# A hybrid decoder layer on one core: the second half's residual norm in the middle of the first FFN block, its steps and the second norm one block further to the front

## The chip, the cores and the metric

The kernel runs on one core of a Trainium2 chip. The metric is the device time of one execution in microseconds (us), lower is better; a median over several executions is given where there are several. A core has TensorE (PE, matmuls, with its weight loads shown as PEld), VectorE (DVE), ScalarE (ACT), GpSimd (POOL) and SyncE (SP), which here only issues transfers. Each engine works through a queue of its own in order, and waits on semaphores for the others.

## The reference

One layer over a sequence of 1024 positions of width 1024, in float32. A token mixer with three branches (pooling, RWKV-7, attention into a memory) gives `merged`; then come an output projection, two norms and a gated feed-forward network with a causal convolution of width 3:

```python
x = x + rms_norm(merged @ w_o[l], norm_mix_post[l])

h = rms_norm(x, norm_ffn_pre[l])
u = causal_dwconv(h @ w_ffn_up[l], conv_w[l], conv_b[l])
u_gate, u_val = jnp.split(u, 2, axis=-1)
f = (jax.nn.gelu(u_gate, approximate=True) * u_val) @ w_ffn_down[l]
x = x + rms_norm(f, norm_ffn_post[l])
```

`rms_norm` divides each position by the root of its mean square over the 1024 channels. The feed-forward width is 2816 for the gate and 2816 for the value. The change lies between the output projection and the first blocks of the feed-forward network.

## The kernel before

Everything is kept transposed: channels on the 128 partitions, positions along the row. The 1024 positions are worked on in two halves of 512 (index n); the 1024 channels are 8 chunks of 128 (index k). Each float32 operand of a matmul is split into a high and a low part, and a product takes three matmuls (`mm3`, lines 163 to 171: high by high, low by high, high by low). A block of the feed-forward's first matrix is 128 output columns for one half: `gemm` (L173) runs 8 chunks of three matmuls, 24 in all, into one PSUM bank.

Weights come through `load_w`: SP loads 128x256 pieces (L158), ScalarE casts the high part (L129) and GpSimd subtracts for the low part (L132). A block has four pieces. Two classes of buffers alternate between blocks, three raw and four split pieces each. So a cast for a block can only run when the matmuls of the block two before it have read the piece in that place.

`up_block` (L978) is one such block and its convolution: ScalarE scales the bank and adds the bias (L962), VectorE adds the two shifted products (L963, L964). Block j below `NF` (22) is a gate block, block `NF` + j its value block. `up_act` (L984) takes the GELU of a gate block, multiplies by the value block and stores the product.

Between the output projection of a half (`wo_gemm`) and its feed-forward blocks stand two norms. `wo_residual(n, after)` is a generator: it asks TensorE for the sum over channels of the squares that `wo_gemm` has collected (L1097 in `norm`, a matmul by a matrix of 1/1024), takes the inverse root on ScalarE (a logarithm and an exponential, both L200), and then for each chunk scales on VectorE (L1140), adds x (L1142), stores the result to `d_x1` on SP (L1143) and adds its square to a second sum (ScalarE L1091, VectorE L1092). It yields after every second chunk, so it has four steps, the first of which includes the norm. `wo_norm(n, s2, after)` is the second norm: again a matmul (L1097) and an inverse root, then for each chunk a scaling (L1159), a cast to the high part (L122) and a subtraction for the low part (L123), the operands `h2h[n]` and `h2l[n]` of the feed-forward blocks of half n. It yields after every second chunk too. In both, `after` keeps the norm's matmul behind a given matmul in TensorE's queue.

The code around the change (L1191 to L1223) runs feed-forward blocks of half 0 while the norms of half 1 go on. The order is: block one (gate 0); norm of the residual, chunks 0 and 1; block two (value 0); chunks 2 and 3; block three (gate 1); chunks 4 and 5; block four (value 1); chunks 6 and 7; blocks five and six (gate 2, value 2); the weights of two blocks ahead; the second norm and its first step; the load of the GELU table; then blocks seven to ten (gate and value 3 and 4), with the gate products of pairs 0, 1 and 2 and the other three steps of the second norm behind blocks seven, eight and nine, and the last two gate products at the end. After that come the five block pairs of half 1 (`early`), which need all of `h2h[1]`, with `differences(k)` (L1252 to L1257, VectorE subtractions L1255 and splits) between them; they prepare operands for the 17 remaining pairs, which use a Strassen-like scheme (`up_pair`), and then comes the second matrix.

This program order is not the order of the queues. The framework that builds the program puts each engine's instructions in order by their place in the program and by when it thinks their inputs are there; `later` and `after` add fixed orders.

Of the kernel before, what the change touches and what calls it, by code (L numbers as in the profile page):

```python
# [20 lines left out]
KC = D // P  # L21
# [7 lines left out]
NF = 22  # L29
# [15 lines left out]
def trunk_kernel(ctx: ExitStack, tc: tile.TileContext, xT, memT, pvec, w_in, w_kv, w_upd, w_upg,  # L45
# [98 lines left out]
    def load_w(ap, nk, kp=2, c=None):  # L144
        if c is None:
            cls[0] ^= 1
            c = cls[0]
        ps = Ws()
        ps.c = c
        for k0 in range(0, nk, kp):  # L150
            load_more(ps, ap, k0, min(kp, nk - k0), kp)
        return ps

    def load_more(ps, ap, k0, n, kp):
        raw = wp.tile([P, kp, P], F32, name="wraw", tag=f"wraw{ps.c}", bufs=3)
        hi = wp.tile([P, kp, P], FR, name="whi", tag=f"whi{ps.c}", bufs=4)
        lo = wp.tile([P, kp, P], FR, name="wlo", tag=f"wlo{ps.c}", bufs=4)
        SP.dma_start(raw[:, :n], ap[:, k0:k0 + n])  # L158
        split_w(raw[:, :n], hi[:, :n], lo[:, :n])
        for j in range(n):  # L160
            ps.append((hi[:, j], lo[:, j]))

    last_mm = [None]

    def mm3(ps, w, x, start, stop):
        wh, wl = w
        xh, xl = x
        first = PE.matmul(ps, wh, xh, start=start, stop=False)  # L168
        PE.matmul(ps, wh, xl, start=False, stop=False)  # L169
        last_mm[0] = PE.matmul(ps, wl, xh, start=False, stop=stop).ins  # L170
        return first

    def gemm(ws, rhs, width=512, behind=None, ps=None, log=None):  # L173

        if ps is None:
            ps = psg.tile([P, 512], F32, name="psg", tag=f"g{getattr(ws, 'c', 0)}")[:, :width]
        n = len(ws)
        for k in range(n):
            m = mm3(ps, ws[k], rhs(k), k == 0, k == n - 1)
            if k == 0 and behind is not None:  # L180
                later(m, behind)
            if log is not None:
                log.append(last_mm[0])
        return ps


# [44 lines left out]
    first = [Ws(), Ws()]  # L231
# [522 lines left out]
    with tc.tile_pool(name="km", bufs=1) as km:  # L754
# [31 lines left out]
        for j in range(8):  # L786
            ws = kv_weights(j) if j > 1 else load_w(w_kv[j], KC, c=0)
            ps = gemm(ws, lambda k: (mh[:, k], ml[:, k]), 256)
# [61 lines left out]
    for hd in range(4):  # L850
        for t0, _ in HALVES:
# [7 lines left out]
            for u in range(2):  # L859
                ps = psg.tile([P, 2, 256], F32, name="psco", tag="g0")  # L860
# [41 lines left out]
    for j in range(8):  # L902
        ws = load_w(w_pmem[j], 4)
        for n, (t0, _) in enumerate(HALVES):
# [3 lines left out]
            ps = gemm(ws, lambda k: (oh[k][:, s], ol[k][:, s]))  # L908
            V.tensor_tensor(pm[j][n], pm[j][n], ps, op=ALU.mult)
    for j in range(8):  # L910
        ws = load_w(w_ppool[j], 4)
# [3 lines left out]
        for n, (t0, _) in enumerate(HALVES):  # L915
            s = slice(t0, t0 + 512)
            ps = gemm(ws, lambda k: (ph_[k][:, s], pl_[k][:, s]))
# [39 lines left out]
    def conv(j, n, src, d):  # L957

        if n == 0:
            zcs[j] = const.tile([P, 2], F32, name="zc2", tag="zc2", bufs=16)  # L960
        zc = zcs[j]
        A.activation(d, src, AF.Identity, scale=col("cw2", j), bias=col("cb", j))  # L962
        V.scalar_tensor_tensor(d[:, 1:], src[:, :511], col("cw1", j), d[:, 1:], op0=ALU.mult, op1=ALU.add)  # L963
        V.scalar_tensor_tensor(d[:, 2:], src[:, :510], col("cw0", j), d[:, 2:], op0=ALU.mult, op1=ALU.add)  # L964
        if n == 0:
            V.tensor_copy(zc, src[:, 510:512])
        else:
            V.scalar_tensor_tensor(d[:, 0:1], zc[:, 1:2], col("cw1", j), d[:, 0:1], op0=ALU.mult,
                                   op1=ALU.add)
            V.scalar_tensor_tensor(d[:, 0:2], zc, col("cw0", j), d[:, 0:2], op0=ALU.mult, op1=ALU.add)  # L970
# [4 lines left out]
        cnt[e] = (cnt[e] + 1) % 4  # L975
        return pmp.tile([P, 512], F32, name=name, tag=f"n{8 + 4 * e + cnt[e]}")

    def up_block(j, n, ws):  # L978
        e = j // NF
        d = work(e, ("ug", "uv")[e])  # L980
        conv(j, n, gemm(ws, lambda k: (h2h[n][:, k], h2l[n][:, k])), d)
        return d

    def up_act(i, n, ug, uv):  # L984
        act(ug, ug, AF.Gelu_apprx_tanh)
        V.tensor_tensor(ug, ug, uv, op=ALU.mult)
        SP.dma_start(d_f[i][:, n * 512:n * 512 + 512], ug)
# [96 lines left out]
    h2h, h2l = [], []  # L1084
# [40 lines left out]
    def wo_residual(n, after=None):  # L1125

        s = slice(n * 512, n * 512 + 512)
        o = os_[n]
        rs = norm(ow, sss[n], after)
        s2 = ow.tile([P, 512], F32, name="s2", tag="ss", bufs=2)  # L1130
        if n:
            xts = hf.tile([P, KC, 512], F32, name="xts", tag="h2h1")
            SP.dma_start(xts, xT[:, s].rearrange("(k p) t -> p k t", p=P))
        for k in range(KC):
            if n:
                xt = xts[:, k]
            else:
                xt = ow.tile([P, 512], F32, name="xt", tag="xt", bufs=2)
                SP.dma_start(xt, xT[k * P:(k + 1) * P, s])
            V.scalar_tensor_tensor(o[k], o[k], col("g_mix_post", k), rs, op0=ALU.mult,  # L1140
                                   op1=ALU.mult)
            V.tensor_tensor(o[k], o[k], xt, op=ALU.add)  # L1142
            SP.dma_start(d_x1[k][:, s], o[k])  # L1143
            sumsq(s2, o[k], k == 0, V)
            if k % 2:
                yield s2
# [6 lines left out]
    def wo_norm(n, s2, after=None):  # L1153

        o = os_[n]
        rs = norm(ow, s2, after)
        new_h2()
        for k in range(KC):
            V.scalar_tensor_tensor(o[k], o[k], col("g_ffn_pre", k), rs, op0=ALU.mult,  # L1159
                                   op1=ALU.mult)  # L1160
            split(o[k], h2h[n][:, k], h2l[n][:, k], V)
            if k % 2:
                yield
# [13 lines left out]
    res = wo_residual(0, pin)  # L1177
    s2 = next(res)
    table(SIGMOID)
    for j in range(3, 8):  # L1180
        merge(1, range(j, j + 1))
        s2 = next(res, s2)
# [5 lines left out]
    for _ in wo_norm(0, s2, last_mm[0]):  # L1188
        pass
    wo_gemm(1, range(2, 8))  # L1190
    def first(j):  # L1191
        return up_block(j, 0, load_w(w_fup[j], KC))

    pairs = [[first(0)]]
    res = wo_residual(1, last_mm[0])
    s2 = next(res)
    pairs[0].append(first(NF))
    s2 = next(res)
    for i in (1, 2):
        pairs.append([first(i)])  # L1200
        s2 = next(res, s2)
        pairs[i].append(first(NF + i))
        s2 = next(res, s2)

    ahead = [load_w(w_fup[3], KC), load_w(w_fup[NF + 3], KC)]
    steps = wo_norm(1, s2, last_mm[0])
    next(steps)
    table(GELU)
    later(phase[0], last_whi[0], True)
    for n in range(4):  # L1210
        j = (3, NF + 3, 4, NF + 4)[n]
        d = up_block(j, 0, ahead.pop(0))
        if n < 2:
            ahead.append(load_w(w_fup[(4, NF + 4)[n]], KC))
            up_act(n, 0, *pairs[n])
            pairs.append([d])
        else:
            up_act(n, 0, *pairs[n]) if n == 2 else None
            pairs.append([d])
        if n < 3:  # L1220
            next(steps)
    up_act(3, 0, pairs[3][0], pairs[4][0])
    up_act(4, 0, pairs[5][0], pairs[6][0])  # L1223


    o0, o1 = os_
# [137 lines left out]
    log = []  # L1364
# [34 lines left out]
    X, ahead, third = down  # L1399
# [217 lines left out]
```

## Time and profile before

| | |
|---|---|
| median of 3 runs | 2079.53 us (2077.59 to 2079.88) |
| the profiled execution, its own time | 2081.88 us |
| its span, first to last instruction | 2080.0 us |
| mean granted TensorE clock | 0.992 |
| TensorE busy, span | 2014.5 us, 97% |
| VectorE, ScalarE, GpSimd busy | 1361.4, 1069.4, 812.5 us |
| TensorE busy, 1372.0 to 1437.6 (half 0's ten blocks) | 61.92 of 65.60 us |
| TensorE busy, 1437.6 to 1500.0 (half 1's ten blocks) | 55.46 of 62.40 us |

The profile is one execution. Times in it are in us from the first instruction. In a row of an engine's queue stand the start, the length, the engine, the line of the kernel, the operation, the tile written and the tiles read, the shapes, how many instructions were joined (x2), and in brackets how long the engine was idle before it and what that wait ended with. In a row by stretches, each engine has its busy time and its number of instructions. Matmuls overlap: one is shown as 0.39 us long, but they start about 0.23 us apart. Tiles of the text have these names there: `psn` is the bank of a norm, `psg` that of a block, `ss` the first sum of squares, `s` the second, `rs` the inverse root, `ug` and `uv` the outputs of gate and value blocks, `o` the output projection and later the residual, `whi`, `wlo` and `wraw` the split and the raw weights.

### The profile page before, as it was taken

The page shows a single profiled execution, that of the slowest core. Times are in us where ns is not written, and L with a number is a line of the kernel's source. Part 1 is how long each engine was busy: PE and PEld are TensorE (multiplying, and loading weights), DVE is VectorE, ACT ScalarE, POOL GpSimd, SP SyncE. Part 2 cuts the span into 40 slices and gives each one's busy share as a digit, 9 for nine tenths or more (in the row PEclk, how much of TensorE's full clock was granted, in tenths as well). Part 3 has the DMA queues.
Part 4 walks back from the last instruction along what each step waited for, and adds up shares of the span by engine and source line. Part 5 has one row for each costly group of instructions (what it writes and reads, how often), then busy time and mean ns, then how long its engine had stood idle before and what let it go on. Part 6 is the DMA issues. An engine that isn't in the chain of part 4 may idle for free.

```text
span 2080.0 us, 34125 instructions
## 1 busy us (share of the span) xinstructions
PE 2014.5 (97%) x12246; PEld 1558.7 (75%) x12246; DVE 1361.4 (65%) x2170; ACT 1069.4 (51%) x2249; POOL 812.5 (39%) x917
## 2 busy tenths in 40 slices
PE   8999999999999999999999999998999999989997
PEld 5777767776778667866878878876678777767886
DVE  6567437664667357823895443778777777767798
ACT  7585348623773367434566243546444443444644
POOL 5521213121222121212133355655588888832341
PEclk9999999999999999999999999999999999999999
DMA  4312211120212021214427343634322222169776
GB/s 155 130 41 74 67 59 61 65 82 22 87 61 98 24 89 61 78 51 133 160 82 234 123 142 110 213 123 135 109 72 76 79 74 83 64 189 261 166 181 149
DMA packets 176713, 221.83 MB, mean 107 GB/s; under 512 B 16544, under 2 KB 128288, under 8 KB 176544
## 3 DMA queue, kind: packets, MB, share of 16 engines
q1 hardware_dynamic: 163616, 204.44, 30.3%
q0 software_dynamic: 11856, 14.16, 4.2%
q8 instruction: 97, 1.59, 0.3%
q10 hardware_dynamic: 1072, 1.05, 0.2%
q14 instruction: 72, 0.59, 0.1%
HBM read 170.30 MB, written 49.28 MB: 106 GB/s over the span
## 4 chain that ended last, share of the span: by engine, by line
PE 30%; DVE 7%; DMA 5%; POOL 4%; issue 4%; ACT 3%; SPq 0%; POOLq 0%; ACTq 0%; DVEq 0%
PE psg L170 5%; PE psg L169 5%; PE psg L168 5%; POOL wt L1028 2%; PE psd L169 2%; PE psd L170 2%; PE psf L170 2%; PE psd L168 2%; PE psf L169 2%; PE psf L168 2%; POOL sm L1013 1%; DMA a<-in_w_fup 1%; DMA g<-d_zg 1%; DMA R<-d_f 1%; POOL wlo L132 1%
## 5 line engine op out<-in xcount | busy, mean ns | idle before, releaser
L132 POOL TENSOR_TENSOR wlo<-wraw,whi 128x256 fp32r<-128x256 f32 x472 | 411.6, 881 | 941.8 <-ACT whi L129 775.1
L168 PE MATMUL psg<-hh,whi 128*128 128x512 f32 x928 | 380.7, 410 | 2.7 <-DVE kv L315 2.7
L170 PE MATMUL psg<-hh,wlo 128*128 128x512 f32 x928 | 376.9, 406 | 0.2
L169 PE MATMUL psg<-hl,whi 128*128 128x512 f32 x928 | 375.8, 405 | 0.0
L129 ACT CAST whi<-wraw 128x256 fp32r<-128x256 f32 x472 | 182.7, 403 | 220.8 <-PE psg L169 108.0
L168 PEld LDWEIGHTS psg<-hh,whi 128*128 128x128 f32 x928 | 174.7, 188 | 43.3 <-DVE kv L315 4.0
L170 PEld LDWEIGHTS psg<-hh,wlo 128*128 128x128 f32 x928 | 174.5, 188 | 43.2 <-POOL wlo L132 5.3
L169 PEld LDWEIGHTS psg<-hl,whi 128*128 128x128 f32 x928 | 174.7, 188 | 39.5 <-issue 3.4
L1028 POOL TENSOR_TENSOR wt<-a,wt 128x256 fp32r<-128x256 f32 x136 | 133.8, 1013 | 31.3 <-ACT wt L1027 31.3
L168 PE MATMUL psd<-f,u 128*128 128x512 f32 x292 | 115.8, 397 | 8.2 <-ACT f L1355 4.8
L169 PE MATMUL psd<-f,u 128*128 128x512 f32 x292 | 115.6, 396 | 0.6 <-DVE f L1359 0.6
L170 PE MATMUL psd<-f,u 128*128 128x512 f32 x292 | 115.2, 396 | 0.0
L1028 POOL TENSOR_TENSOR wt<-sm,wt 128x256 fp32r<-128x256 f32 x102 | 106.8, 1066 | 19.2 <-ACT wt L1027 19.2
L170 PE MATMUL psf<-h2h,wt 128*128 128x512 f32 x272 | 108.8, 400 | 1.0 <-POOL wt L1028 0.6
L168 PE MATMUL psf<-h2h,wt 128*128 128x512 f32 x272 | 106.3, 391 | 1.7 <-ACT wt L1027 1.6
L169 PE MATMUL psf<-h2l,wt 128*128 128x512 f32 x272 | 106.0, 390 | 0.0
L1027 ACT CAST wt<-sm 128x256 fp32r<-128x256 f32 x102 | 37.9, 404 | 129.4 <-POOL sm L1013 124.1
L1046 DVE SCALAR_TENSOR_TENSOR d<-z,pv,d 128x1023 f32<-128x1023 f32 x68 | 91.6, 1347 | 12.0 <-ACT d L1044 9.5
L170 PE MATMUL psf<-t,wt 128*128 128x512 f32 x204 | 80.8, 396 | 3.4 <-POOL wt L1028 3.4
L686 DVE TENSOR_TENSOR HV<-ph,Hd 64x128 f32<-64x128 f32 x112 | 32.4, 289 | 72.2 <-PE ph L640 48.0
L168 PE MATMUL psf<-t,wt 128*128 128x512 f32 x204 | 79.6, 390 | 0.0
L169 PE MATMUL psf<-t,wt 128*128 128x512 f32 x204 | 79.5, 390 | 0.0
(424 smaller groups left out, 4750.7 us busy)
## 6 DMA issues: line engine op xcount, KB each, us to landing
wraw<-in_w_in SPq DMA_DIRECT2D x240, 128.0 KB, 2.4
a<-in_w_fup SPq DMA_DIRECT2D x128, 128.0 KB, 2.4
d_zg<-st SPq DMA_DIRECT2D x48, 256.0 KB, 2.7
wraw<-in_w_fup SPq DMA_DIRECT2D x80, 128.0 KB, 2.5
fw<-in_w_fdn SPq DMA_DIRECT2D x33, 256.0 KB, 4.2
fraw<-d_f SPq DMA_DIRECT2D x33, 256.0 KB, 5.3
wraw<-in_w_prwkv SPq DMA_DIRECT2D x64, 128.0 KB, 2.4
wraw<-in_w_o SPq DMA_DIRECT2D x64, 128.0 KB, 2.5
```

The lines of the kernel that those rows point to most:

```text
L129: last_whi[0] = A.copy(hi, src).ins
L132: (V if lo_on_dve[0] else G).tensor_tensor(lo, src, hi.bitcast(F32), op=ALU.subtract)
L168: first = PE.matmul(ps, wh, xh, start=start, stop=False)
L169: PE.matmul(ps, wh, xl, start=False, stop=False)
L170: last_mm[0] = PE.matmul(ps, wl, xh, start=False, stop=stop).ins
L686: ready = V.tensor_tensor(HV[q, :, c + 1, e], ph[q], Hd[q], op=ALU.add).ins
L1013: eng.tensor_tensor(out_[u], a[u], b[u], op=op)
L1027: A.copy(w[0][:, us], src[u])
L1028: last_low[0] = G.tensor_tensor(w[1][:, us], src[u], w[0][:, us].bitcast(F32), op=ALU.subtract).ins
L1046: V.scalar_tensor_tensor(d[:, n:], z[:, :T - n], col(cw, j), d[:, n:], op0=ALU.mult, op1=ALU.add)
```

## The change

`gemm` gets an argument `amid`, a function that it calls behind the matmuls of chunk 3, and `up_block` passes it on. The start of `wo_residual(1)` with its norm and chunks 0 and 1 becomes such a function of block one, and the norm's matmul is kept behind the 12th matmul of the block instead of the 24th. Of the other steps, chunks 2 and 3 now come ahead of block two, 4 and 5 ahead of block three, 6 and 7 ahead of block four. The second norm comes behind block five instead of six: blocks six to ten are now in `queue`, the first two of them (value 2 and gate 3) have their weights loaded ahead, and the gate products of pairs 0, 1 and 2 with the three steps of the second norm follow blocks six, seven and eight. Number, operands and shapes of all operations stay.

```diff
-    def gemm(ws, rhs, width=512, behind=None, ps=None, log=None):
+    def gemm(ws, rhs, width=512, behind=None, ps=None, log=None, amid=None):
...
             if log is not None:
                 log.append(last_mm[0])
+            if amid is not None and k == 3:
+                amid()
         return ps
...
-    def up_block(j, n, ws):
+    def up_block(j, n, ws, amid=None):
         e = j // NF
         d = work(e, ("ug", "uv")[e])
-        conv(j, n, gemm(ws, lambda k: (h2h[n][:, k], h2l[n][:, k])), d)
+        conv(j, n, gemm(ws, lambda k: (h2h[n][:, k], h2l[n][:, k]), amid=amid), d)
         return d
...
-    def first(j):
-        return up_block(j, 0, load_w(w_fup[j], KC))
-
-    pairs = [[first(0)]]
-    res = wo_residual(1, last_mm[0])
-    s2 = next(res)
-    pairs[0].append(first(NF))
-    s2 = next(res)
-    for i in (1, 2):
-        pairs.append([first(i)])
-        s2 = next(res, s2)
-        pairs[i].append(first(NF + i))
-        s2 = next(res, s2)
-
-    ahead = [load_w(w_fup[3], KC), load_w(w_fup[NF + 3], KC)]
-    steps = wo_norm(1, s2, last_mm[0])
+    blocks, s2 = [], [None]
+
+    def first(j, amid=None):
+        blocks.append(up_block(j, 0, load_w(w_fup[j], KC), amid))
+
+    def begin():
+        res.append(wo_residual(1, last_mm[0]))
+        s2[0] = next(res[0])
+
+    res = []
+    first(0, begin)
+    for j in (NF, 1, NF + 1, 2):
+        s2[0] = next(res[0], s2[0])
+        first(j)
+
+    queue = (NF + 2, 3, NF + 3, 4, NF + 4)
+    ahead = [load_w(w_fup[j], KC) for j in queue[:2]]
+    steps = wo_norm(1, s2[0], last_mm[0])
     next(steps)
     table(GELU)
     later(phase[0], last_whi[0], True)
-    for n in range(4):
-        j = (3, NF + 3, 4, NF + 4)[n]
-        d = up_block(j, 0, ahead.pop(0))
-        if n < 2:
-            ahead.append(load_w(w_fup[(4, NF + 4)[n]], KC))
-            up_act(n, 0, *pairs[n])
-            pairs.append([d])
-        else:
-            up_act(n, 0, *pairs[n]) if n == 2 else None
-            pairs.append([d])
+    for n, j in enumerate(queue):
+        blocks.append(up_block(j, 0, ahead.pop(0)))
         if n < 3:
+            ahead.append(load_w(w_fup[queue[n + 2]], KC))
+            up_act(n, 0, *blocks[2 * n:2 * n + 2])
             next(steps)
-    up_act(3, 0, pairs[3][0], pairs[4][0])
-    up_act(4, 0, pairs[5][0], pairs[6][0])
+    for n in (3, 4):
+        up_act(n, 0, *blocks[2 * n:2 * n + 2])
```

## The prediction

> **What bounds the kernel now.** I read the page first, then busy time by stretches around the edited code, then the queues of TensorE, VectorE and ScalarE there, and the waits last.
>
> ```profile
> span 2080.0 us, 34125 instructions
> ...
> PE 2014.5 (97%) x12246; PEld 1558.7 (75%) x12246; DVE 1361.4 (65%) x2170; ACT 1069.4 (51%) x2249; POOL 812.5 (39%) x917
> ...
> PE 30%; DVE 7%; DMA 5%; POOL 4%; issue 4%; ACT 3%; SPq 0%; POOLq 0%; ACTq 0%; DVEq 0%
> ```
>
> TensorE is busy for 97% of the span, so only its gaps can be won. The second view gives busy time and counts by stretch; the columns after POOL are granted clock, DMA share and GB/s.
>
> ```profile
> 1372.00:1405.60 33.60, 33.60 (x147) 27.14 (x145) 23.49 (x33) 14.43 (x33) 19.20 (x23) 1.00 0.47 147
> 1405.60:1412.60 7.00, 3.32 (x7) 1.88 (x7) 5.11 (x10) 4.15 (x10) 4.54 (x6) 0.76 0.59 191
> 1412.60:1437.60 25.00, 25.00 (x112) 20.53 (x110) 20.33 (x31) 15.59 (x32) 13.58 (x14) 1.00 0.48 147
> 1437.60:1460.00 22.40, 18.55 (x73) 13.01 (x73) 22.09 (x30) 12.89 (x29) 14.61 (x15) 1.00 0.27 88
> 1460.00:1480.00 20.00, 18.64 (x77) 13.63 (x76) 18.61 (x28) 9.61 (x23) 11.77 (x15) 1.00 0.36 114
> ```
>
> Two stretches lose TensorE time: 1405.6 to 1412.6, and 1437.6 to 1480, where VectorE is busy for 40.7 of 42.4 us. TensorE's own queue shows the first:
>
> ```profile
> 1372.03 0.39 PE L168 MATMUL psg<-h2h,whi 128*128 128x512 f32 x1
> ...
> 1377.24 0.40 PE L170 MATMUL psg<-h2h,wlo 128*128 128x512 f32 x1
> 1377.47 1.02 PE L1097 MATMUL psn<-ss,ones 128*128 128x512 f32 x2
> ...
> 1378.80 0.40 PE L170 MATMUL psg<-h2h,wlo 128*128 128x512 f32 x1
> ...
> 1405.37 0.40 PE L170 MATMUL psg<-h2h,wlo 128*128 128x512 f32 x1
> 1409.45 2.08 PE L1097 MATMUL psn<-s,ones 128*128 128x512 f32 x2 [3.68 <-DVE s L1092]
> 1410.54 1.42 PE L168 MATMUL psg<-h2h,whi 128*128 128x512 f32 x1
> ...
> 1412.48 0.40 PE L168 MATMUL psg<-h2h,whi 128*128 128x512 f32 x1
> ```
>
> A block is 24 matmuls; from the first to the last of block one (1372.03 to 1377.24) there are 23 steps, so 0.2265 us each and 5.44 us a block. The norm's matmul costs 0.88 us: 1377.24 to 1378.80 is 1.56 for what would be three steps, 0.68. The second norm's matmul could have gone at 1405.60 and went at 1409.45. Without a stall the matmul at 1412.48, four steps and one norm behind 1405.37, would have been at 1407.16: 5.3 us are lost, 3.85 in the wait and 1.45 in what follows it (slow matmuls, clock below). By the same step the 73 and 77 matmuls of the two later stretches need 16.5 and 17.4 us and have 22.4 and 20.0: 8.4 us lost, a little less if records are missing. These 13.7 us are all that the edit can reach.
>
> **The change, part by part.** No arithmetic, transfer or byte is added or taken out. Three things move: the first norm's matmul goes from behind block one into its middle; each of the four residual steps goes one block further to the front; the second norm goes from behind block six to behind block five, and with it the GELU table load, the h2 steps and the first three gate products.
>
> The VectorE queue, the ScalarE queue and its waits give the prices:
>
> ```profile
> 1373.68 0.69 DVE L1121 TENSOR_TENSOR ss<-ss,sq 128x512 f32<-128x512 f32 x1
> 1384.15 0.75 DVE L963 SCALAR_TENSOR_TENSOR ug<-psg,pv,ug 128x511 f32<-128x511 f32 x1 [9.78 <-ACT ug L962]
> ...
> 1385.67 1.89 DVE L1140 SCALAR_TENSOR_TENSOR o<-o,pv,rs 128x512 f32<-128x512 f32 x2
> ...
> 1389.23 1.90 DVE L1140 SCALAR_TENSOR_TENSOR o<-o,pv,rs 128x512 f32<-128x512 f32 x2
> ...
> 1407.58 1.81 DVE L1092 TENSOR_TENSOR s<-s,sq 128x512 f32<-128x512 f32 x2
> ...
> 1418.77 2.07 DVE L1159 SCALAR_TENSOR_TENSOR o<-o,pv,rs 128x512 f32<-128x512 f32 x3
> ```
>
> ```profile
> 1378.51 1.33 ACT L129 CAST whi<-wraw 128x256 fp32r<-128x256 f32 x4 [3.22 <-PE psn L1097]
> 1383.03 0.41 ACT L129 CAST whi<-wraw 128x256 fp32r<-128x256 f32 x1 [3.19 <-DMA wraw<-in_w_fup]
> 1383.34 0.78 ACT L962 ACTIVATE ug<-psg,pv 128x512 f32<-128x512 f32 x1
> 1384.02 0.68 ACT L200 ACTIVATE rs<-psn,eps 128x512 f32<-128x512 f32 x1
> 1384.73 0.63 ACT L200 ACTIVATE rs<-rs 128x512 f32<-128x512 f32 x1
> ...
> 1416.13 0.41 ACT L129 CAST whi<-wraw 128x256 fp32r<-128x256 f32 x1 [4.11 <-PE psg L170]
> 1416.44 0.78 ACT L962 ACTIVATE uv<-psg,pv 128x512 f32<-128x512 f32 x1
> 1417.12 0.68 ACT L200 ACTIVATE rs<-psn,eps 128x512 f32<-128x512 f32 x1
> ```
>
> *First norm.* Its input is complete at 1373.68 + 0.69 = 1374.37. After 12 matmuls of block one its turn is 1372.03 + 12 x 0.2265 = 1374.75, so TensorE does not wait; the cover is thin, 0.4 us, and if it were gone every us would be a us of TensorE. The 0.88 us are paid in either place. The result was there at 1378.49, but ScalarE began the logarithm only at 1384.02: in its queue stood four weight casts, one more that waited 3.19 us for its weights, and block one's bias step. That last cast and the bias step need the end of block one (the cast reuses the buffer that the last matmuls read), and the norm now comes before that. So I place logarithm and exponential (1.34 us, 1384.02 to 1385.36) ahead of them, behind three of the four casts, at about 1379.5, and the scale is ready at 1380.8 instead of 1385.36.
>
> *Residual.* VectorE took 23.7 us from 1385.67 to 1409.39 (of its 23.49 busy us in the first stretch at most 2.4 can lie before 1374.37, so at least 21.1 of the 21.45 from 1384.15 to 1405.60 are busy), with three blocks' convolutions (1.52 us each, 1384.15 to 1385.67) in between. Now the first four operations (3.56 us, up to 1389.23) run from 1380.8 to 1384.4, then block one's convolution to 1385.9, then the rest: 1409.39 - 1389.23 = 20.16, less block four's convolution, which the earlier start leaves behind: 18.6. The sum is complete at 1404.5; with that convolution it would be 1406.
>
> *Second norm on TensorE.* Five blocks and one norm from 1372.03 end at 1372.03 + 5 x 5.44 + 0.88 = 1400.1. So TensorE waits 4.4 us instead of 3.85: the wait is not removed, since its place moved by a whole block and its input by 4.9 us. Counted in work done, the old start behind five blocks is 1409.45 - 5.44 = 1404.0, the new one 1404.5: 0.5 us lost. Queued behind the waiting matmul are blocks six to ten and, through the banks, their convolutions.
>
> What follows a wait differs. The stretch from 1405.6 has clock 0.76 over 7.0 us, which is half clock for 3.4 us. Another wait of nearly that length stands late in the kernel, with its stretch and its matmul:
>
> ```profile
> 1843.50:1850.40 6.90, 6.82 (x18) 5.16 (x19) 6.81 (x9) 4.76 (x6) 1.29 (x1) 0.59 1.08 367
> ```
>
> ```profile
> 1843.58 0.80 PE L168 MATMUL psd<-f,u 128*128 128x512 f32 x1 [4.14 <-ACT f L1355]
> ```
>
> After 3.68 us without work the slow clock cost 1.45; after 4.14 us the clock was 0.59 over 6.9 us, so half for 5.7, and 18 matmuls took 6.9 us instead of 4.1: 2.8 lost. For 4.4 us I take half of the 1.4 between them, 0.7, and keep both ends. The Trainium skill, "TensorE: Matmul & The Clock Gate" (part 1, the two states), has the array at half clock after an idle window of about 3.4 us and back after one busy window of the same length. By that rule alone the longer wait would cost nothing more, and the sum below would be 0.7 us lower; the second row speaks against it, or shows a window only partly busy.
>
> *Second scale and second half.* The second logarithm stood at 1417.12 behind a cast and a bias step of block six, 7.7 us after the norm's start. Behind block five there is one cast group fewer to wait for, but its last cast again needs a buffer freed late, so I put the logarithm about 1410 and VectorE's norm steps at 1411.9 instead of 1418.77: VectorE gains 6.9 us on the clock, TensorE arrives 1.2 us later. The later loss is a chain of weights behind these steps:
>
> ```profile
> ACT t L122 <- DVE o L1255: 10.8, 8, 3.9
> ...
> PE psg L170 <- POOL wlo L132: 2.7, 4, 1.6
> PE psg L168 <- ACT whi L129: 2.2, 4, 1.3
> ```
>
> ScalarE waits for VectorE's differences with weight casts queued behind, and TensorE for those. VectorE's headroom grows by 6.9 + 1.2 = 8.1 us, but if the queue orders follow the program, the differences also move one block (5.44) ahead among the weight casts, and 2.7 remain. The other end is the whole 8.1 of the 8.4 lost. I take 3.5, near the lower end, since the second norm's program place does move by that block; nothing excludes a loss of 1 us from other casts falling behind.
>
> *Transfers.* The issues between 1325 and 1450 (KB, us to landing) and SP's own waits there:
>
> ```profile
> xts<-in_xT SPq DMA_DIRECT2D x1, 2048.0 KB, 7.9
> d_x<-o SPq DMA_DIRECT2D x8, 256.0 KB, 2.6
> ```
>
> ```profile
> SPq L1143 <- DVE o L1142: 3.1, 4, 1.3
> ```
>
> The 2 MB of x land in 7.9 us, long before they are used. The eight stores go earlier among the weight loads; each that SP reaches before VectorE is done holds the loads behind it: 3.1 us in four cases before, covered by buffers for nearly two blocks. I cost the move at nothing; with that cover gone it is up to 1.3 us a store. POOL gets no instruction and is moved past none.
>
> The sum: +0.5 +0.7 -3.5 = -2.3 us. The profiled execution took 2081.88 us, 2.35 above the median of the runs, so 2079.6 by its own count and 2077.2 as a median.
>
> **Rivals.** *A, both stalls go.* If ScalarE's queue has the logarithm ahead of the casts that start at 1378.51, where it idles for 3.22 us, it begins at 1374.75 + 1.02 = 1375.8, the scale is there at 1377.1 and the sum at 1400.8: a wait of 0.7 us, too short for the clock. That is -3.2 - 1.45 - 3.5 = -8.1, 2071.4; nearly the same comes out where the logarithm is as forecast and the later stretch recovers 7 us. For it: the idle time is there. Against: two of those casts need only the first half of block one and are ahead in the program. *B, slower.* If the logarithm stays behind the cast of 1383.03, only block one's bias step is saved: scale at 1383.34 + 1.34 = 1384.7, sum at 1408.4, and TensorE, called one block earlier, waits 8.3 us. That is +4.4, +1.4 for the clock, and at most -1 later: +4.8, 2084.3. It decides at a scale later than about 1383.5, and the change then turns a wait into a longer one. For it: the norms before sat behind such casts twice (1384.02, 1417.12). *C, nothing moves.* The framework orders each engine's queue itself, so the residual can run where it ran, with matmul and VectorE shifted alike: 2079.5 give or take 2.
>
> **How the numbers follow.** Forecast (gain 0 to 5) 0.5, A 0.24, B 0.16, C 0.1. A measurement of this kernel can tell about 0.2% (4.2 us) from no change. Faster by more: A and a tenth of the forecast's chance, 0.29; slower by more: most of B, 0.15; within: 0.56. The range leaves out A's far half and B's far half: 2071 to 2084.5; the forecast's own is 2074.5 to 2080.
>
> **What would show it.** Right: in the changed profile the first norm's matmul starts near 1374.8 without idle time, the first scale's logarithm near 1379.5, the last sum of squares ends near 1404.5, TensorE still waits 4 to 5 us for it, now behind five blocks, the second logarithm is near 1410, and between 1437 and 1480 TensorE loses about 5 us instead of 8.4. Wrong: no wait at the second norm (A), one of 7 us or more (B), or the stretch after 1437 as lossy as before.

## The result, and the profile after

The changed kernel took 2074.52 us (median of 7 runs, 2069.57 to 2075.8) beside 2079.53 for the kernel before (7 runs, 2077.59 to 2082.5): a ratio of 0.9968, 95% interval 0.9957 to 0.998. Measured once more among the experiments, it was 2073.29 beside 2076.45: 0.9983, 0.9973 to 0.9993. So it is faster, by 3 to 7 us by the two ratios, which is about the 0.2% that one measurement can tell. The profiled execution has a span of 2072.5 us and its own time is 2074.52.

The page of the changed kernel, its span and busy times:

```profile
span 2072.5 us, 34127 instructions
...
PE 2011.6 (97%) x12246; PEld 1560.3 (75%) x12246; DVE 1357.0 (65%) x2170; ACT 1068.5 (52%) x2249; POOL 813.8 (39%) x917
```

As many matmuls and VectorE operations as before, and TensorE still at 97%. But of the 7.5 us between the two spans only some are the edit's. Block one starts at 1370.70 instead of 1372.03, ahead of everything that was edited, and 4.0 us arise between 1831.7 and 1881.9 (times of the kernel before), where the instruction orders of all engines are the same. So I measure from the start of block one to the first matmul of the Strassen-like part, `psf` (below: the stretch). It holds all that the edit can move. The two ends, in TensorE's queue of the kernel before and of the changed one:

```profile
1499.74 0.47 PE L168 MATMUL psf<-h2h,wt 128*128 128x512 f32 x1
```

```profile
1370.70 0.39 PE L168 MATMUL psg<-h2h,whi 128*128 128x512 f32 x1
...
1373.42 1.02 PE L1099 MATMUL psn<-ss,ones 128*128 128x512 f32 x2
...
1398.59 0.39 PE L170 MATMUL psg<-h2h,wlo 128*128 128x512 f32 x1
1404.39 2.07 PE L1099 MATMUL psn<-s,ones 128*128 128x512 f32 x2 [5.41 <-DVE s L1094]
1405.47 1.42 PE L168 MATMUL psg<-h2h,whi 128*128 128x512 f32 x1
...
1495.32 0.39 PE L168 MATMUL psf<-h2h,wt 128*128 128x512 f32 x1
```

The stretch is 1499.74 - 1372.03 = 127.71 us before and 124.62 after: 3.1 us shorter. Second profiles of both give 128.87 and 124.80, 4.1 shorter. The first norm's matmul sits in block one without a wait; at the second norm TensorE is idle for longer than before (5.41 us in the bracket instead of 3.68). Busy time by stretches, in the same columns and the same five pieces as before:

```profile
1372.00:1405.60 33.60, 28.19 (x120) 22.31 (x119) 24.65 (x37) 16.31 (x38) 19.56 (x24) 0.97 0.51 161
1405.60:1412.60 7.00, 7.00 (x22) 5.18 (x21) 2.43 (x5) 3.53 (x5) 1.41 (x2) 0.67 0.71 200
1412.60:1437.60 25.00, 25.00 (x112) 20.72 (x111) 25.00 (x35) 15.94 (x36) 15.86 (x15) 1.00 0.42 128
1437.60:1460.00 22.40, 20.42 (x87) 15.70 (x86) 22.36 (x30) 12.22 (x28) 15.20 (x15) 1.00 0.28 86
1460.00:1480.00 20.00, 19.49 (x84) 15.50 (x84) 13.49 (x24) 10.82 (x27) 12.25 (x16) 1.00 0.41 128
```

The wait has moved into the first piece, the slow clock (0.67 over 7 us) is in the second, and the last two hold 171 matmuls instead of 150. In 42.4 us there is room for 187, so 3.6 us are lost there instead of 8.4. ScalarE and VectorE show why the second scale was not earlier still:

```profile
1377.20 1.02 ACT L129 CAST whi<-wraw 128x256 fp32r<-128x256 f32 x3 [3.18 <-DMA wraw<-in_w_fup]
1378.13 0.68 ACT L202 ACTIVATE rs<-psn,eps 128x512 f32<-128x512 f32 x1
...
1409.02 0.41 ACT L129 CAST whi<-wraw 128x256 fp32r<-128x256 f32 x1 [4.64 <-PE psg L170]
1409.33 0.77 ACT L964 ACTIVATE ug<-psg,pv 128x512 f32<-128x512 f32 x1
1410.01 0.68 ACT L202 ACTIVATE rs<-psn,eps 128x512 f32<-128x512 f32 x1
```

```profile
1402.99 0.75 DVE L965 SCALAR_TENSOR_TENSOR uv<-psg,pv,uv 128x511 f32<-128x511 f32 x1 [0.75 <-ACT uv L964]
1403.65 0.68 DVE L1094 TENSOR_TENSOR s<-s,sq 128x512 f32<-128x512 f32 x1
...
1411.66 2.07 DVE L1161 SCALAR_TENSOR_TENSOR o<-o,pv,rs 128x512 f32<-128x512 f32 x3
```

The sum of squares is complete at 1404.33. ScalarE then stands 4.64 us at a weight cast of block seven, and the logarithm is two places behind it. The row names a matmul as what ended that wait; SP's queue and the table of transfers from 1400 to 1410 say that it was the weights:

```profile
1403.96 0.42 SPq L1310 DMA_DIRECT2D fw<-in_w_fdn  x1
1404.94 0.33 SPq L158 DMA_DIRECT2D wraw<-in_w_fup  x1
```

```profile
fw<-in_w_fdn SPq DMA_DIRECT2D x3, 256.0 KB, 4.6
wraw<-in_w_fup SPq DMA_DIRECT2D x5, 128.0 KB, 4.0
```

The piece was issued at 1404.94 and landed 3.98 us later, at 1408.92; the cast began at 1409.02. The Trainium skill, "TensorE: Matmul & The Clock Gate" (the table at its head), calls the queues of ScalarE, VectorE and GpSimd strictly first in, first out. This row agrees: the norm's matmul began 5.6 us before the logarithm that reads it.

### The profile page after: what moved, and what is told of

It reads as the page before. It is cut to its first block, busy times and chain, and to the rows that moved or that the text cites. A ratio compares the mean times of both kernels' runs of the same rounds, so it can differ in the third digit from the quotient of the medians.

```text
span 2072.5 us, 34127 instructions
## 1 busy us (share of the span) xinstructions
PE 2011.6 (97%) x12246; PEld 1560.3 (75%) x12246; DVE 1357.0 (65%) x2170; ACT 1068.5 (52%) x2249; POOL 813.8 (39%) x917
## 4 chain that ended last, share of the span: by engine, by line
PE 28%; DVE 7%; DMA 6%; POOL 5%; issue 3%; ACT 3%; SPq 1%; POOLq 0%; ACTq 0%; DVEq 0%
PE psg L170 5%; PE psg L168 5%; PE psg L169 5%; POOL wt L1030 3%; PE psd L169 2%; PE psd L170 2%; PE psd L168 2%; PE psf L170 2%; PE psf L168 2%; PE psf L169 2%; DMA a<-in_w_fup 1%; POOL sm L1015 1%; DMA R<-d_f 1%; ACT d L1046 1%; DMA g<-d_zg 1%
## 5 line engine op out<-in xcount | busy, mean ns | idle before, releaser
L1029 ACT CAST wt<-sm 128x256 fp32r<-128x256 f32 x102 | 37.9, 404 | 129.1 <-POOL sm L1015 124.2
```

The source lines that it names most:

```text
L1029: A.copy(w[0][:, us], src[u])
```

## The experiments

Each kernel was timed in rounds with the kernel before on the same chip. Medians of before were 2076.76 us (first four), 2076.45 (second four) and 2077.05 (last four); ratios compare within a group. Times of events below are counted from the start of block one, so that the shift ahead of it drops out.

**One part at a time.** The first expectations set theory T (the gain comes from the first scale's place in ScalarE's queue, and the second norm's move alone costs) against U (the gain comes from the second norm's place, and what the first part wins at the norm is lost again in half 1's blocks).

The first norm amid block one and the residual's steps moved, the second norm still behind block six (shown against the changed kernel):

```diff
-    for j in (NF, 1, NF + 1, 2):
+    for j in (NF, 1, NF + 1, 2, NF + 2):
...
-    queue = (NF + 2, 3, NF + 3, 4, NF + 4)
+    queue = (3, NF + 3, 4, NF + 4)
...
```

> The first part of the change alone: the first norm in the middle of block one and the residual steps one block further to the front, while the second norm stays behind block six as before. Theory T (the gain comes from the first scale's place in ScalarE's queue, ahead of a weight cast that waits for its transfer): the scale is ready about 4.6 us earlier, the second sum ends 4 to 5 us earlier, TensorE calls it only behind six blocks, so the wait of 3.85 us and the slow clock behind it (1.45 us) are gone; the stretch of half 1's blocks stays about as lossy as before (8.6 us), or up to 3 us more since TensorE arrives earlier. Net 2.5 to 5.5 us faster than before. Theory U (the gain comes from the second norm's place, which lets VectorE start on half 1's operands 7 us earlier): what is won at the norm is lost again in the blocks of half 1; net 0 to 2 us faster.

Measured: 2074.05 us, 0.9986 (0.9978 to 0.9995). The wait at the second norm shrank to 0.80 us and the clock stayed full, but the stretch is 126.73, only 1.0 to 2.1 us shorter. TensorE came to half 1 no earlier than before (61.7), because it waited twice in block nine for split weights (0.8 and 1.2 us) and ran at half clock from 1420.14 to 1423.56; the second scale was hardly earlier (VectorE's second-norm steps at 45.6 instead of 46.7), and half 1's blocks lost nearly as much as before. The time lies in T's range (2.5 to 5.5 us faster), the stretch does not.

Only the second norm moved, behind block five:

```diff
-    first(0, begin)
-    for j in (NF, 1, NF + 1, 2):
-        s2[0] = next(res[0], s2[0])
+    first(0)
+    begin()
+    for j in (NF, 1, NF + 1):
...
+        s2[0] = next(res[0], s2[0])
+    first(2)
```

> The other part alone: first norm and residual steps stay where they were before, the second norm comes behind block five instead of six. Theory T: the sum ends as before (about 32 us behind the first norm), TensorE calls it 5.4 us earlier, so it waits about 9 us instead of 3.85 and runs 1.4 us longer at the slow clock; about 2 to 4 us come back in half 1's blocks. Net 2 to 5 us slower than before. Theory U: VectorE starts on half 1's operands earlier by what the second logarithm is, and half 1's blocks lose 4 us or more less; net 1 to 4 us faster than before.

Measured: 2073.87 us, 0.9985 (0.9976 to 0.9994). T expected 2 to 5 us slower and fell. TensorE's and ScalarE's queues of this kernel:

```profile
1405.15 2.08 PE L1099 MATMUL psn<-s,ones 128*128 128x512 f32 x2 [8.79 <-DVE s L1094]
```

```profile
1405.70 0.40 ACT L129 CAST whi<-wraw 128x256 fp32r<-128x256 f32 x1 [1.74 <-POOL wlo L132]
1406.01 0.77 ACT L964 ACTIVATE ug<-psg,pv 128x512 f32<-128x512 f32 x1
1407.26 0.69 ACT L202 ACTIVATE rs<-psn,eps 128x512 f32<-128x512 f32 x1 [0.47 <-PE psn L1099]
```

TensorE waits 8.8 us, the longest of all, and the stretch is nevertheless 124.18, as short as the changed kernel's. The cast ahead of the logarithm waits only 1.74 us and is done before the norm, so that the logarithm goes as soon as the norm is there (39.2, as in the changed kernel, though the sum is 3.4 us later); and half 1's blocks run almost without a stall. Busy time from 1436 to 1478 (68 to 110 from block one), which is half 1:

```profile
1436.00:1458.00 22.00, 22.00 (x99) 18.22 (x98) 21.97 (x32) 12.85 (x28) 15.60 (x16) 1.00 0.29 89
1458.00:1478.00 20.00, 20.00 (x90) 16.57 (x89) 11.68 (x23) 9.22 (x22) 10.88 (x15) 1.00 0.41 131
```

VectorE is as full as before in the first piece, TensorE loses nothing. What was paid at the norm was paid back. By the stretch this part alone gives what the whole edit gives (3.5 to 4.7 us against 3.1 to 4.1); by the times the two parts can't be told apart (0.9986 and 0.9985).

**The kernel before with one cast behind the first scale.** No move, only the cast of 1383.03 pinned behind the first exponential:

```diff
+    scale = phase[1][-1]
...
+        if i == 1:
+            later(last_whi[0], scale, True)
```

> The kernel before with one fixed order added: the last weight cast of block three comes behind the first norm's exponential in ScalarE's queue (before it stood ahead of it and waited 3.19 us for its weights). TensorE's queue is untouched. Theory T: logarithm at about 1380.5 instead of 1384.0 us, the sum about 3.5 us earlier, the wait at the second norm falls from 3.85 us to below 0.5 and the clock stays up; net 2.5 to 5 us faster than before, about what the first part alone gives. Theory U: as good as nothing, 0 to 1 us faster.

Measured: 2073.43 us, 0.9984 (0.9974 to 0.9995), stretch 125.23: first logarithm at 8.4 instead of 12.0, wait at the second norm 1.73 us with the clock full, second-norm steps at 43.6. One cast, moved behind a bias step and the two instructions of the inverse root, makes the stretch 2.5 to 3.6 us shorter, the whole edit 3.1 to 4.1. That is in T's range, and U, which expected 0 to 1 us, fell as well: neither place alone explains the gains.

**The second norm in the middle of a block.** The changed kernel with `wo_norm(1)` begun amid block six:

```diff
-    steps = wo_norm(1, s2[0], last_mm[0])
-    next(steps)
...
+    def second():
+        steps.append(wo_norm(1, s2[0], last_mm[0]))
+        next(steps[0])
...
-        blocks.append(up_block(j, 0, ahead.pop(0)))
+        blocks.append(up_block(j, 0, ahead.pop(0), second if n == 0 else None))
...
```

> The change with one more step: the second norm too is asked for in the middle of its block, behind the 12th matmul of block six. It tests the price of the longer wait that the change makes at the second norm (5.6 us in the profile of the changed kernel, with half clock for some 6.8 us behind it). Both theories agree on the sum's end. If that wait and the clock behind it cost TensorE what the step times say (8.4 us), a call 2.7 us later leaves a wait of 2.9 us and at most 1.5 us of slow clock: 4 us faster than the changed kernel, 9 to 11 us faster than before. If instead the end is set by VectorE and the casts in half 1's blocks, the later call gives 0 to 1 us against the changed kernel.

Measured: 2070.71 us, 0.9969 (0.9958 to 0.998), stretch 123.49. The wait fell to 3.33 us, but TensorE came to half 1 only 1.0 to 1.9 us earlier than in the changed kernel, and the stretch is only 1.1 to 1.3 us shorter, nearer to the 0 to 1 us of the second case than to 4.

**Theory V and its rival W.** After these, V said: what counts is when VectorE begins the second norm's steps; from there it works without a gap to the end of the differences, 81 us before the end of the stretch. W said: TensorE pays its wait whatever ScalarE does, and weight casts hold half 1. The changed kernel again, beside three more:

> The changed kernel again, beside the three kernels of this group, as their base on the same chip. Every theory: the same 2.5 to 7 us below the kernel before as the first time (ratio 0.996 to 0.998); its second profile shows which of the local times repeat: TensorE waits 5 to 6 us at the second norm, the second logarithm 39 to 40 us behind the start of block one, VectorE's second-norm steps at 41, the loss in half 1's blocks about 4 us.

Measured: 2073.29 us, 0.9983; wait 5.59, second logarithm 39.2, steps 40.9: the local times repeat. The same with block seven's last cast behind the second exponential:

```diff
+    later(last_whi[0], phase[1][-1], True)
```

> The changed kernel, with one weight cast (the last piece loaded ahead, of block seven) put behind the second norm's exponential in ScalarE's queue. Theory V (what counts is when VectorE begins the second norm's steps, since from there it works without a gap to the end of the differences; the early sum of the changed kernel is wasted behind that cast): the second logarithm 35 to 36.5 us behind the start of block one instead of 39.3, VectorE's steps at 37 to 38 instead of 41, the loss in half 1's blocks 0 to 2 us instead of 4, in all 2 to 4 us faster than the changed kernel. Rival W (TensorE is held by the norm's sum and pays its wait whatever ScalarE does; half 1's blocks are held by weight casts, not by VectorE): the logarithm moves, the sum of the losses does not, within 1 us of the changed kernel; the late cast may add 1 us at block seven.

Measured: 2069.49 us, 0.9967 (0.9954 to 0.998), 3.8 below the changed kernel beside it. ScalarE's and VectorE's queues:

```profile
1407.85 0.69 ACT L202 ACTIVATE rs<-psn,eps 128x512 f32<-128x512 f32 x1 [1.30 <-PE psn L1099]
1408.57 0.63 ACT L202 ACTIVATE rs<-rs 128x512 f32<-128x512 f32 x1
1410.88 0.40 ACT L129 CAST whi<-wraw 128x256 fp32r<-128x256 f32 x1 [1.68 <-DMA wraw<-in_w_fup]
```

```profile
1409.24 2.07 DVE L1161 SCALAR_TENSOR_TENSOR o<-o,pv,rs 128x512 f32<-128x512 f32 x3 [1.06 <-ACT rs L202]
```

Block one began at 1371.44, so logarithm and steps are at 36.4 and 37.8, as V had it, 3 us earlier than in the changed kernel. But the stretch is 123.63, only 1.0 to 1.2 shorter, which is about W's 1 us, and half 1's blocks still lost 3.2 us, where V had 0 to 2. So of the 3.8 us some are not accounted for by the stretch (the two intervals overlap), and V's fixed 81 us failed: from the steps it was 85.8.

> The first experiment's second kernel (only the second norm moved, behind block five), with the second norm's matmul in the middle of block six instead. TensorE arrives 12 matmuls, 2.7 us, later, so its wait is 6.3 us instead of about 9. Theory V: VectorE's second-norm steps begin where they did (40 to 41 us behind the start of block one), so that the end of half 1's blocks does not move: 0 to 1 us against the kernel with the norm behind block five; the loss only moves from the wait to half 1's blocks. Rival W: TensorE wins the 2.7 us, with the loss in half 1's blocks staying near 0, 2 to 3 us faster.

The edit is that of the kernel with the norm in the middle of block six, made to the kernel with only the second norm moved. Measured: 2072.34 us, 0.998 (0.9967 to 0.9992), stretch 123.89, against 124.18: the wait fell from 8.8 to 6.6 us, half 1's blocks took 1.0 us more. That is V's case (the loss moves), not W's.

> The changed kernel with the second norm in the middle of block six, and the cast of block seven's last piece behind its exponential: both in one. Theory V: second logarithm at 36 to 37.5 us behind the start of block one, VectorE's steps at 38 to 39, both the wait at the second norm (3 to 4 us instead of 5.6) and the loss in half 1's blocks (0 to 2) shrink: 2 to 5 us faster than the changed kernel. Rival W: 1 to 2.7 us faster, all of it from the shorter wait, as in the kernel with the norm in the block alone (2070.7).

Both edits in the changed kernel (norm amid block six, cast behind its exponential). Measured: 2065.85 us, 0.9956 (0.9939 to 0.9973), stretch 119.55, which is 5.1 to 5.3 shorter than the changed kernel's. The time is 7.4 us below the changed kernel beside it, more than V (2 to 5) and W (1 to 2.7) had; the wait (3.9 us), the logarithm, the steps and half 1's loss (2.0 us) are where V had them. On another chip:

> The kernel with the norm in the middle of block six and the cast behind the second exponential, again, as base for the next one and on another chip: 6 to 11 us below before (ratio 0.995 to 0.997); in its profile a stretch of 119 to 120.5 us from block one to the first Strassen matmul (119.55 the first time).

2067.5 us, 0.9958 (0.9945 to 0.9972), stretch 120.67, a little over the expected 120.5. Here TensorE waited 2.56 us with the clock full and came to half 1 2.5 us earlier, but half 1 lost 6.0 us instead of 2.0. This is the best version: 9 us below the kernel before by both ratios, and 4 to 5 us shorter than the changed one by the stretch (7.4 us by the medians of the one group that has both).

> The kernel before once more, for a second profile of it. If the local times are the edit's and not the execution's: second logarithm 45 us behind the start of block one, VectorE's second-norm steps at 46.7, a loss of 5 to 6 us at the second norm and of 8 to 9 in half 1's blocks, and the first Strassen matmul 127 to 128.5 us behind the start of block one (127.7 in the first profile; 124.6 and 124.8 in the two of the changed kernel). If it is nearer 125, the local gain was one execution's too.

One run, 2074.82 us, stretch 128.87 (127.71 the first time), second-norm steps at 47.9. The local loss did not repeat in its parts: the wait was 3.06 us with the clock full, and TensorE waited 1.2 us for a split weight in block nine instead. Its span is 2073.0, 7 us shorter than the first profile's, although the stretch is 1.2 longer: two spans of one kernel differ by more than the edit is worth, while the stretch repeats to 1.2 us.

**VectorE's work itself.** The kernel before with the third tap left out in half 1's ten early blocks, and the same edit in the best version:

```diff
-        V.scalar_tensor_tensor(d[:, 2:], src[:, :510], col("cw0", j), d[:, 2:], op0=ALU.mult, op1=ALU.add)
+        if n == 0:
+            V.scalar_tensor_tensor(d[:, 2:], src[:, :510], col("cw0", j), d[:, 2:], op0=ALU.mult, op1=ALU.add)
```

> The kernel before without the third tap of the convolution in half 1's ten early blocks (ten VectorE operations of 0.66 us left out, 6.6 us; the output lacks that term there). Theory V (in the kernel before, VectorE from the second norm's steps to the end of the differences sets the end of the stretch): the stretch gets 4 to 6.6 us shorter, 121 to 123.5 instead of 127.7, the loss in half 1's blocks 2 to 5 us instead of 8.7. Rival W (weights and casts hold TensorE there, VectorE is only beside them): 0 to 1.5 us, loss in half 1's blocks 7 us or more.

Measured: 2074.85 us, 0.9991 (0.9979 to 1.0003), stretch 125.97: of 6.6 us only 1.7 to 2.9, between V's 4 to 6.6 and W's 0 to 1.5; half 1 lost 9.9 us, as W had it. V in its strong form is out. TensorE's waits in half 1, of this kernel and, below, of the changed one:

```profile
PE psg L170 <- POOL wlo L132: 3.1, 5, 1.6
PE psg L168 <- ACT whi L129: 1.8, 3, 1.3
PE psg L170 <- DVE wlo L132: 0.4, 1, 0.4
```

```profile
PE psg L170 <- POOL wlo L132: 1.8, 2, 1.2
PE psg L170 <- DVE wlo L132: 0.7, 1, 0.7
PE psg L168 <- ACT whi L129: 0.6, 2, 0.4
```

VectorE's last difference ended at 96.5 instead of 101.3 and 102.9, and TensorE waited for split weights as it had before (POOL 2.7, ACT 2.2 us).

> The same ten VectorE operations left out of the kernel with the norm in the middle of block six and the late cast (the output lacks the same term). Theory V with its second bound (there VectorE no longer sets the end; TensorE is held by the sum of squares at the second norm, and no engine can give that back): the stretch stays within 1.2 us of 119.6, with the 7 us lost at the second norm in place, time within 2 us of that kernel. Rival W, or V without the second bound: as much as in the kernel before, 4 us or more.

Measured: 2067.47 us, 0.9964 (0.9951 to 0.9977) beside 2067.5 for the same kernel with the tap; stretch 120.46. As V with its second bound had it; but since the same work was worth little in the kernel before too, this no longer speaks for that bound.

**What is left.** One relation goes through all the profiles. Arrival is when TensorE starts the first block of half 1 (the 241st block matmul), steps when VectorE starts the second norm's scaling, both from block one; head is their difference; half 1 is the time from the 241st to the 480th matmul, 54.2 us without a loss (239 x 0.2266).

| kernel | arrival | steps | head | half 1 | stretch |
|---|---|---|---|---|---|
| before; again | 61.5; 62.8 | 46.7; 47.9 | 14.8; 14.9 | 65.7; 65.9 | 127.7; 128.9 |
| before, tap left out | 61.7 | 46.6 | 15.1 | 64.1 | 126.0 |
| before, cast behind first scale | 59.1 | 43.6 | 15.5 | 65.9 | 125.2 |
| first part alone | 61.7 | 45.6 | 16.1 | 64.4 | 126.7 |
| changed, norm amid block six | 62.8 | 42.3 | 20.5 | 60.2 | 123.5 |
| changed; again | 64.7; 63.7 | 41.0; 40.9 | 23.7; 22.9 | 59.7; 60.8 | 124.6; 124.8 |
| best version; again | 62.8; 60.3 | 38.7; 37.4 | 24.2; 22.9 | 56.1; 60.2 | 119.6; 120.7 |
| best version, tap left out | 62.1 | 37.2 | 24.9 | 58.1 | 120.5 |
| second part alone, norm amid block six | 66.0 | 41.3 | 24.7 | 57.1 | 123.9 |
| second part alone | 67.8 | 40.6 | 27.3 | 56.1 | 124.2 |
| changed, cast behind second scale | 65.4 | 37.8 | 27.6 | 57.3 | 123.6 |

Half 1 takes about 65 us at a head of 15 and 56 to 57 at one of 27, about 0.7 us less for each us of head (a straight line through the 14 profiles, with a scatter of 1 us and once 2.4). So a later arrival is mostly paid back in half 1, and steps that begin earlier win where the arrival stays. It is a relation between kernels, and no run changes the head alone. One rival can be set aside: with the second norm earlier, the differences' casts also stand one block further to the front among the weight casts, but in the changed kernel and in the second part alone they stand in the same places, and there half 1 still differs by 3.6 to 4.7 us at a head that differs by 3.6 to 4.4. The work that VectorE does in half 1 is not the measure of it, nor is the wait that I had named as the chain, ScalarE's for the differences. From 55 to 110 us, in the changed kernel, the one with the second part alone, and the kernel before without the tap:

```profile
ACT t L122 <- DVE o L1253: 10.2, 5, 3.6
```

```profile
ACT t L122 <- DVE o L1255: 8.3, 5, 2.6
```

```profile
ACT t L122 <- DVE o L1256: 7.2, 6, 2.4
```

Half 1 lost 5.6, 2.0 and 9.9 us in these, and 11.5 in the kernel before, where that wait was 10.8: ScalarE's wait hardly changes, or goes the other way. Which link turns the head into TensorE's loss (the weights' landing, the free buffers, the casts' places) stays open; putting the weight casts ahead of the differences' casts would have told more and was not tried.

## Why the prediction was right or wrong

The path was right and the direction too: the wait at the second norm stays and grows a little, and half 1 gives back more. The forecast of -2.3 us was small beside the -3.1 and -4.1 of the two pairs of stretches. That the sum came so near is partly luck: in the first pair TensorE arrived 1.9 us later than forecast and half 1 gave back 2.5 us more, and the two misses cancel. The medians differ by 5.0 us, of which the stretch holds 3.1. The likeliest class (within 0.2%) was the wrong one for the first comparison, -0.32% with an interval that ends at -0.2%, and the right one for the second, -0.17%.

- *First norm*: as forecast. Its matmul at 1373.42 is 2.72 us behind the start of block one, the forecast's 1374.75 - 1372.03; no wait. The logarithm came behind three of the four casts at 7.43, forecast 7.5.
- *Residual*: the sum ended at 33.6, forecast 32.5, or 34 with one more convolution. That convolution did get in front: one of its taps (0.75 us) and the 0.75 us wait for its bias step are the rows at 1402.99.
- *Second norm on TensorE*: right in kind, mis-sized. The wait is 1404.39 - 1398.59 - 0.23 = 5.57 us instead of 4.4, by the same convolution. *Clock*: 3.0 us lost behind the wait, at the upper of the two ends (2.8), where 2.15 was taken; 2.0 in the second profile. Which of the two comes is chance: the wait was the same, but half clock ended 5.9 us behind the start of the norm's matmul in the first and 3.8 in the second, by where the clock's fixed times fell (last section). Together TensorE arrives at half 1 3.1 us later (1.0 in the second pair), forecast 1.2.
- *Second scale*: the logarithm at 39.3, forecast 38; VectorE's steps at 41.0, forecast 39.9, so 5.8 us earlier than before (7.0 in the second pair) instead of 6.9. The forecast has 1.9 us from logarithm to steps, where the rows of before give 1418.77 - 1417.12 = 1.65, as in the changed kernel; that slip hid 0.25 us. The logarithm stood behind a cast whose weights came late; the text had looked for a late buffer there.
- *Second half*: the step that was mis-sized most. The head grew by 8.9 and 8.0 us, forecast 8.1, and the differences did move one block ahead among the weight casts, as assumed. But I subtracted that block, 5.44 us, nearly whole and took 3.5; half 1 got back 6.0 and 5.1. The subtraction took each us of ScalarE's wait at the differences for a us of TensorE's. ScalarE's wait is nearly what it was (10.2 and 9.3 us, 10.8 before), and TensorE's loss is about half (5.6 and 6.6 us, 11.5 and 11.7 before). The 8.4 us that the prediction set as the limit stop at 1480; to its end half 1 lost 11.5.
- *Rivals*: A (both stalls go) did not happen here, since the wait grew; its second case, in which the later stretch gives back 7 us, was nearer than the forecast's 3.5 in the first pair (6.0) and not in the second (5.1). B needed a scale later than 1383.5; it was ready at 1379.47, 8.8 us from block one where B begins at 11.5. Its mechanism was seen without its price: with the second norm alone moved TensorE did wait 8.8 us, and lost nothing in the end, because half 1 gave it back. That is what B and the forecast's sum both missed: the terms are not independent. C is out, since the orders moved as the program did.
- *Transfers* at nothing: the moved stores added no stall: SP waited 0.8 us at them in all, 3.1 before. But a transfer sets the second scale, by the piece issued at 1404.94; in the kernel before the cast in that place had waited 4.11 us too.

## What to carry to other kernels

When TensorE stalls twice, the first stall need not be a plain cost: here it gave the other engines a head start, and where it grew or shrank the second stall went the other way, by about 0.7 us for each us of head. Ask for each term whether a later stretch gives it back, and gain by starting the late chain earlier at the same arrival: here by taking one cast that waits for its weights out of the way of an inverse root, which together with the norm asked for in mid-block took 4 to 5 us more off the stretch than the edit alone. And where single spans scatter by 7 us, measure the edited stretch from a fixed event in two profiles of each kernel.

## What the runs showed of the hardware

The slow clock behind a wait goes by fixed times and not by the wait's length. In all 14 profiles the granted clock changes only at times that lie a whole number of 3.413 us apart, wherever the waits are: in the changed kernel it is half from 1403.42 to 1410.24, two such pieces, and then full for 125 of them, to 1836.91. Three pieces of the best version without the tap, around a wait of 2.69 us at the second norm, and two of the second profile of before, around one of 3.06 us:

```profile
1398.20:1401.61 3.41, 1.35 (x6) 0.77 (x5) 3.28 (x7) 1.87 (x4) 0.98 (x2) 1.00 0.36 123
1401.61:1405.02 3.41, 2.79 (x5) 1.57 (x6) 2.86 (x6) 2.70 (x7) 3.20 (x5) 0.50 0.71 224
1405.02:1408.44 3.42, 3.42 (x10) 2.68 (x9) 2.71 (x4) 3.36 (x6) 1.37 (x2) 0.50 0.94 282
```

```profile
1402.11:1405.52 3.41, 1.86 (x6) 0.90 (x6) 3.41 (x7) 2.21 (x5) 1.53 (x2) 1.00 0.47 149
1405.52:1408.93 3.41, 1.72 (x6) 1.12 (x7) 1.54 (x3) 1.64 (x5) 2.58 (x3) 1.00 0.50 157
```

In the first, TensorE was idle for 2.06 us of one piece, and the next two have half clock. In the second the longer wait is cut by the time 1405.52 into pieces with 1.55 and 1.69 us of idle, and the clock stayed full. Around the 14 second norms, a piece at full clock with 1.96 us of idle or more was followed by half clock each time, one with 1.58 or less never, and between them (1.69 twice, 1.73) both occurred; half clock ended behind a piece with 0.55 us of idle or less and went on behind one with 0.62 or more. So waits of 1.73, 2.56 and 3.06 us could keep the full clock, and one of 2.69 ran at half clock for 6.2 us behind it, longer than one of 8.79 (5.4 us). The Trainium skill, "TensorE: Matmul & The Clock Gate" (part 1, the two states), has half clock after an idle window of about 3.4 us and full clock after one busy window; the traces agree on the length, but a window brought half clock with TensorE idle for little more than half of it (1.96 us of 3.41).
